# Stick-breaking attention in a two-layer transformer: VectorE and the DMA queue keep the program's order, filler steps are spread over the last units, and one more key tile is loaded before the next stage

## The chip, the core and the metric

The kernel runs on one core of a Trainium2 chip. The metric is device microseconds of one execution. A core has five engines with an instruction queue each: TensorE (PE in the profile; PEld is its weight load), VectorE (DVE), ScalarE (ACT), GpSimd (POOL) and SyncE (SP), which here issues nearly all transfers. Each engine takes its instructions in the order in which they stand in its queue; an instruction that must wait holds up those behind it on the same engine.

## What is computed

Two transformer layers on 2048 tokens of width 1024, float32. The first layer mixes three kinds of heads: six of stick-breaking attention, six of differential attention, four that attend to a memory of 256 rows. The second has sliding-window attention and memory attention. Each layer ends with a gated output projection and a layer norm. The part at issue is stick-breaking attention, here in the reference's words:

```python
def one_block(bi):
    qi = lax.dynamic_slice_in_dim(q, bi * BLOCK, BLOCK, axis=1)
    z = jnp.einsum('bqhd,bkhd->bhqk', qi, k, preferred_element_type=jnp.float32) * scale
    q_idx = bi * BLOCK + jnp.arange(BLOCK, dtype=jnp.int32)
    strict = key_idx[None, :] < q_idx[:, None]
    log_1mb = jnp.where(strict, jax.nn.log_sigmoid(-z), 0.0)
    rc = jnp.flip(jnp.cumsum(jnp.flip(log_1mb, axis=-1), axis=-1), axis=-1)
    after = rc - log_1mb
    w = jnp.where(strict, jnp.exp(jax.nn.log_sigmoid(z) + after), 0.0)
    return jnp.einsum('bhqk,bkhd->bqhd', w.astype(v.dtype), v)
```

A key's weight is its own sigmoid times the product of (1 - sigmoid) over all keys between it and the query. The kernel computes that product as a running product from the last key to the first.

## The kernel before, in words

The stages follow each other: projections of layer 1 (`layer1_proj`), stick-breaking, differential attention (`differential`), the output projection, layer 2.

**Units.** Stick-breaking works on three pairs of heads (p), for each on four chunks of 512 queries (t = 3, 2, 1, 0), and in a chunk on blocks of 128 queries against up to 512 keys. One block against one stretch of keys, for both heads of the pair, is a unit; there are 120. `begin` runs at a chunk's first unit: it loads the chunk's gate (`sl`), the next chunk's queries (`qs`) and, once per pair, the next pair's keys and values (`kv`, three tiles per pair).

**One unit.** `scores`: TensorE multiplies queries and keys into PSUM (`psz`). `weights`: ScalarE takes the two sigmoids (tiles `s` and `wb`), VectorE runs the product scan for each head (`row`), GpSimd multiplies `wb` by it. `turn`: TensorE transposes `wb` into PSUM (`pstp`, two buffers), and the result is copied to `wT`, in turn two copies by ScalarE and one by VectorE. `values`: TensorE multiplies `wT` with the values (`pspv`). The main loop for unit k writes: scores of unit k+3, turn of unit k, weights of unit k+3, and, every second k, the values of two units that were turned before. At a chunk's end VectorE multiplies with `sl` and a store writes `m1` (short: m).

**The filler.** The six stick-breaking heads' and memory heads' share of the output projection is spread over the differential stage as filler. Its first list of steps makes ready: load(0) (mp tile of m1), five loads of w_out parts (`rx`, three buffers), five `wsplit` (ScalarE casts rx into `wo`, GpSimd subtracts for the low part), split(0) and load(1). Thirteen steps in all. `begin` runs them when p = 2 and t = 1 (`FT`), fifteen units before the stage's end, and then loads the differential stage's first queries (`qa`) and keys (`kc`, tile number c for keys 512c on).

**What sets the order.** A scheduler reorders the instructions of each engine by its own model of time, except those that a `PinnedCore` marks to keep the program's order. In stick-breaking TensorE and ScalarE are so marked; VectorE, GpSimd and SP are not. While the filler's first steps are recorded, `self.nc = nc` takes the mark off for all engines. The differential stage marks TensorE and ScalarE.

**Memory.** A tile tag has a fixed number of buffers in a pool; a new tile waits until the oldest one's last user is done. Pools that are opened after others were closed lie where those lay.

Of the kernel before, what the change touches and what calls it, by code (L numbers as in the profile page):

```python
# [15 lines left out]
S = 2048  # L16
D = 1024
# [49 lines left out]
class Net:  # L67
# [152 lines left out]
    def load_x(self, between):  # L220

        nc = self.nc
        self.xs = []
        for t in range(NT):
            row = []
            for h in range(2):
                tag = "kv" if 2 * t + h < 3 else "qs" if t < 2 else "big"
                hi, lo = (self.t(tag, F32R, [P, 2048]) for _ in range(2))
                n = 1024 if t or h else 512
                for c in range(0, 2048, n):  # L230
                    raw = self.t("w")[:, :n]
                    self.dma(raw, self.i["xT"][t, h, :, c:c + n])
                    nc.scalar.copy(hi[:, c:c + n], raw)
                    nc.vector.tensor_sub(lo[:, c:c + n], raw, hi[:, c:c + n].bitcast(F32))
                    for f in between.get((t, h, c), ()):
                        f()
                row.append((hi, lo))
            self.xs.append(row)
# [290 lines left out]

    def load_sb(self, p):  # L530

        ks = [self.t("kv", F32R) for _ in range(2)]
        n = S if p else TC
        for lo in range(S - n, -1, -n):
            for hh in range(2):
                for part in range(2):
                    self.dma(ks[hh][64 * part:64 * part + 64, lo:lo + n], self.sbk[p][part, 64 * hh:64 * hh + 64, lo:lo + n])
        vp = self.t("kv", F32, [P, NB, P])
        self.dma(vp, self.v1[:, :, p * P:(p + 1) * P].rearrange("b k f -> k b f"))
        return ks, vp  # L540

    def stick_breaking(self):
# [1 line left out]


        nc = self.nc
        self.nc = pinned = PinnedCore(nc, self.tc, ("tensor", "scalar"))
        chunks = [(p, t) for p in range(3) for t in range(NT - 1, -1, -1)]
        units = [(p, t, qi, c) for p, t in chunks for qi in range(3, -1, -1) for c in range(t, -1, -1)]
        kv, qs, sls, prs, zs, ws, wTs, pvs = {0: self.sb_first[:2]}, {(0, NT - 1): self.sb_first[2]}, {}, {}, {}, {}, {}, {}  # L550
# [1 line left out]
        def begin(p, t):  # L552
            sls[p, t] = self.load_silu(self.silu[p], t)
            k = chunks.index((p, t)) + 1
            if k < len(chunks):
                qs[chunks[k]] = self.load_qstack(self.sbq[chunks[k][0]], chunks[k][1])
            if t == NT - 2 and p < 2:
                kv[p + 1] = self.load_sb(p + 1)
            if p == 2 and t == FT:
                self.fill = self.filler()  # L560
                self.nc = nc
                for f in next(self.fill):
                    f()
                self.nc = pinned
                self.dk, self.dq = {}, {}
                self.load_dq(0, 0, 0)
                for c in range(NT - 1):
                    self.load_dk(0, c)

        def bounds(u):  # L570
# [23 lines left out]
        def weights(u):  # L594
# [6 lines left out]
            self.nc.scalar.activation(w[:, :, :m], z[:, :, :m], AF.Sigmoid, scale=0.125)  # L601
            for hh in range(2):
                prr = prs[p, t, qi][hh]
                nc.vector.tensor_tensor_scan(  # L604
                    prr[:, lo + s0 - 1:hi - 1][:, ::-1], rest[:, hh, s0:m][:, ::-1], zero.to_broadcast([P, m - s0]),
                    prr[:, hi - 1:hi], ALU.mult, ALU.add)
                nc.gpsimd.tensor_mul(w[:, hh, :m], w[:, hh, :m], prr[:, lo:hi])  # L607
# [6 lines left out]
        def values(u):  # L614
# [8 lines left out]
                                          wT[hh][:, j * P:(j + 1) * P], start=(hi == n and j == 0), stop=(c == 0 and j == nj - 1))  # L623
            if qi == 0 and c == 0:
                mt = self.t("c2")
                nc.vector.tensor_mul(mt, pvs.pop((p, t)), sls.pop((p, t)))
                self.dma(self.m1[p, :, t * TC:(t + 1) * TC], mt, nc.scalar if p == 2 and t == 0 else None)

        done = 0
        zero = self.psum("zero")[:, :1]  # L630
        nc.vector.memset(zero, 0.0)
        for u in units[:SB_AHEAD]:
# [2 lines left out]
        for k, u in enumerate(units):  # L635
# [2 lines left out]
            turn(u)  # L638
            if k + SB_AHEAD < len(units):
                weights(units[k + SB_AHEAD])  # L640
            while k - done >= SB_GROUP or k == len(units) - 1 and done <= k:
                for v in units[done:done + SB_GROUP]:
                    values(v)
# [3 lines left out]
    def differential(self):  # L647
# [21 lines left out]
                f()  # L669
            del steps[:k]  # L670

        self.load_dk(0, NT - 1)
        for c in range(NT):
            self.load_dv(0, c)
        for s in range(-2, len(units)):
# [735 lines left out]

    def run(self):
        nc, dr, i = self.nc, self.dr, self.i
        with self.phase({"kv": 6, "qs": 2}, {}):
            with self.phase({"big": 8, "w": 13, "c2": 9, "mv": 2}, {"mm": 3, "z": 2, "tp": 2, "pv": 1}):
                self.layer1_proj()
            right = ExitStack()
            right.enter_context(self.phase({"rx": 3, "mp": 5, "wo": 5, "kc": 3, "qa": 2}, {}, "right"))
            with self.phase({"row": 4, "wb": 4, "s": 3, "wT": 7, "c2": 2, "sl": 2}, {"z": 2, "tp": 2, "pv": 1, "zero": 1}, "right"):
                self.stick_breaking()  # L1420
        self.rp = dr.tile([NB, P, D], F32, name="rp")
        self.silu2 = [dr.tile([P, S], F32, name=f"silu2_{f}") for f in range(8)]
        self.m2 = dr.tile([8, P, S], F32, name="m2")
        with self.phase({"c2": 3, "sl": 2}, {}):
            with self.phase({"qd": 2, "wT": 7, "vc": 4, "row": 9, "kd": 3},
                            {"mm": 1, "z": 3, "tp": 2, "pv": 2}):
                tail = self.differential()
            right.close()
            with self.phase({"big": 16}, {}):
                with self.phase({"w": 4, "raw": 1}, {"mm": 5, "tp": 3}):  # L1430
# [85 lines left out]
```

## Time and profile before

| | |
|---|---|
| Median of 3 runs | 2563.76 us (2556.67 to 2565.95) |
| Profiled execution, its own time | 2562.38 us |
| Its span, first to last instruction | 2560.5 us |
| TensorE busy | 2394.9 us, 94% |
| VectorE busy | 1572.5 us, 61% |
| ScalarE busy | 1253.9 us, 49% |
| GpSimd busy | 942.9 us, 37% |
| Mean transfer rate | 122 GB/s |

Stick-breaking takes 720 to 1082 us of the span, differential attention about 1082 to 1640. A timeline row reads: start, duration (us), engine, source line, operation, tile written <- tiles read, shape, how many; in brackets the idle time before it and what ended it. A row of stretches gives, for each engine, the busy microseconds and in parentheses the number of instructions, then the granted TensorE clock, the share of time that the DMA engines are busy, and GB/s. A row of waits names engine and tile that waited, what it waited for, then microseconds in total, times, longest. L57 is the line of the helper that marks an instruction; such instructions are told apart by their tiles.

### The profile page before, as it was taken

What the parts mean: (1) busy time and instruction counts of PE and PEld (TensorE: products, weight loads), DVE (VectorE), ACT (ScalarE), POOL (GpSimd) and SP (SyncE); (2) the same over time, 40 slices, a digit from 0 to 9 for tenths busy, and PEclk for the clock granted to TensorE, in tenths of its full rate; (3) what the DMA queues carried; (4) which work ended last, traced back from release to release, by engine and by line L of the source; (5) the groups of instructions that cost most, each with busy time, mean ns of one, the idle gap of its engine ahead of it and who ended that gap; (6) DMA issues with size and microseconds to landing.
All of it is one profiled execution on the core that took longest, in us unless ns stands there. A gap on an engine that the chain in (4) does not pass through costs nothing. (4 is left out here: it accounts for less than half of the span.)

```text
span 2560.5 us, 42280 instructions
## 1 busy us (share of the span) xinstructions
PE 2394.9 (94%) x15564; PEld 1942.7 (76%) x15564; DVE 1572.5 (61%) x3657; ACT 1253.9 (49%) x2453; POOL 942.9 (37%) x800
## 2 busy tenths in 40 slices
PE   8999999999969999879888888999999999999998
PEld 7778998888848777657666666778788777777887
DVE  4833222431149888789898999685312776677455
ACT  4442222221138788657687677543212777776100
POOL 0401003750038778610121122374621655534333
PEclk9999999999989999989899999999999999999999
DMA  8643222331481422263534341563323555533541
GB/s 291 205 159 128 81 85 85 126 132 47 122 205 43 108 67 54 64 171 97 129 99 112 94 104 54 173 212 110 87 91 114 154 161 154 145 98 103 197 143 64
DMA packets 199247, 311.60 MB, mean 122 GB/s; under 512 B 17920, under 2 KB 97280, under 8 KB 198528
## 3 DMA queue, kind: packets, MB, share of 16 engines
q1 hardware_dynamic: 198464, 307.83, 40.7%
q8 instruction: 124, 2.03, 0.3%
q10 hardware_dynamic: 576, 1.05, 0.1%
q14 instruction: 83, 0.68, 0.1%
HBM read 204.74 MB, written 104.07 MB: 121 GB/s over the span
## 5 line engine op out<-in xcount | busy, mean ns | idle before, releaser
L57 PE MATMUL psmm<-big,w 128*128 128x512 f32 x1680 | 414.5, 394 | 0.0
L57 PEld LDWEIGHTS psmm<-big,w 128*128 128x128 f32 x1680 | 306.1, 189 | 57.8
L57 ACT COPY wT<-pstp 128x512 f32<-128x512 f32 (+3 forms) x400 | 203.2, 525 | 190.9 <-PE pstp L57 186.6
L607 POOL TENSOR_TENSOR wb<-wb,row 128x512 f32<-128x512 f32 (+3 forms) x240 | 262.5, 1119 | 69.0 <-DVE row L604 49.1
L604 DVE TENSOR_TENSOR_SCAN row<-s,row,pszero 128x512 f32<-128x512 f32 (+5 forms) x240 | 252.2, 1102 | 38.8 <-ACT s L57 37.2
L254 PE MATMUL psmm<-big,w 128*128 128x512 f32 x1200 | 275.2, 389 | 0.0
L254 PEld LDWEIGHTS psmm<-big,w 128*128 128x128 f32 x1200 | 225.0, 188 | 47.0 <-issue 0.2
L57 PE MATMUL psmm<-big,mp 128*128 128x512 f32 x1056 | 244.9, 392 | 1.4 <-POOL big L1011 1.4
L57 ACT ACTIVATE row<-row,mn 128x2048 f32<-128x2048 f32 (+7 forms) x192 | 229.7, 1201 | 12.0 <-DVE mn L777 8.4
L57 PEld LDWEIGHTS psmm<-big,mp 128*128 128x128 f32 x1056 | 198.4, 189 | 42.9 <-POOL big L1011 1.8
L771 DVE TENSOR_SCALAR_CACHE_REDUCE row<-psz 128x512 f32<-128x512 f32 (+1 forms) x324 | 200.5, 639 | 30.6 <-PE psz L57 29.8
L1230 DVE TENSOR_TENSOR c<-psmm,c 128x512 f32<-128x512 f32 x62 | 42.7, 691 | 238.6 <-ACT c L1229 238.5
L941 POOL TENSOR_TENSOR mp<-mp,mp 128x640 fp32r<-128x640 f32 x32 | 53.3, 1667 | 357.4 <-ACT mp L57 268.9
L57 PE MATMUL psz<-kv,qs 128*128 128x512 f32 (+3 forms) x480 | 134.9, 399 | 17.7 <-ACT wb L57 17.4
L57 PE MATMUL psmm<-wo,mp 128*128 128x512 f32 x480 | 148.1, 421 | 3.5 <-ACT mp L57 2.8
L813 DVE SCALAR_TENSOR_TENSOR row<-row,tiny,row 128x128 f32<-128x128 f32 (+7 forms) x144 | 149.8, 1089 | 0.4
L209 POOL TENSOR_TENSOR w<-w,w 128x1024 fp32r<-128x1024 f32 x20 | 48.7, 2437 | 257.1 <-ACT w L208 156.4
L1229 ACT ACTIVATE c<-psmm 128x512 f32<-128x512 f32 x62 | 36.8, 596 | 212.5 <-PE psmm L254 204.2
L57 PE MATMUL pstp<-ident,wb 128*128 128x128 f32 x816 | 117.3, 278 | 24.9 <-DVE wT L125 13.8
L57 PE MATMUL pstp<-ident,row 128*128 128x128 f32 x816 | 131.0, 282 | 7.0 <-ACT wT L57 6.2
L57 PEld LDWEIGHTS pstp<-ident,wb 128*128 128x128 f32 x816 | 92.9, 142 | 45.1 <-POOL wb L607 25.1
L1187 ACT ACTIVATE e<-e,tiny 128x256 f32<-128x256 f32 (+1 forms) x192 | 94.6, 494 | 60.4 <-DVE e L1185 59.8
(220 smaller groups left out, 4923.0 us busy)
## 6 DMA issues: line engine op xcount, KB each, us to landing
silu<-c SPq DMA_DIRECT2D x54, 256.0 KB, 2.3
sl<-silu SPq DMA_DIRECT2D x54, 256.0 KB, 3.2
qs<-sbq SPq DMA_DIRECT2D x48, 256.0 KB, 5.3
cs<-rope SPq DMA_DIRECT2D x24, 512.0 KB, 4.3
kc<-k SPq DMA_DIRECT2D x36, 320.0 KB, 5.0
w<-in_we_dram SPq DMA_DIRECT2D x20, 512.0 KB, 3.7
raw<-in_wo_dram SPq DMA_DIRECT2D x20, 512.0 KB, 4.0
rx<-in_x_dram SPq DMA_DIRECT2D x32, 256.0 KB, 2.8
```

The lines of the kernel that those rows point to most:

```text
L57: return self.tc.keep_in_program_order(f(*a, **k))
L209: eng.tensor_sub(lo[:, sl], raw[:, sl], hi[:, sl].bitcast(F32))
L254: self.nc.tensor.matmul(ps, w[a][:, c, :], self.xpart(t, c, b), start=(c == k == 0), stop=(c == 7 and k == 2))
L604: nc.vector.tensor_tensor_scan(prr[:, lo + s0 - 1:hi - 1][:, ::-1], rest[:, hh, s0:m][:, ::-1], zero.to_broadcast([P, m - s0]), prr[:, hi ...
L607: nc.gpsimd.tensor_mul(w[:, hh, :m], w[:, hh, :m], prr[:, lo:hi])
L771: nc.vector.tensor_scalar(e[:, col + lo:col + lo + n0], z[:, :n0], -scale, before, ALU.mult, ALU.min, accum_out=acc)
L813: self.nc.vector.scalar_tensor_tensor(x[:, lo:hi], y[:, lo:hi], cf[hh][:, w:w + 1], x[:, lo:hi], ALU.mult, ALU.add)
L941: self.nc.gpsimd.tensor_sub(ml, m, mh.bitcast(F32))
L1187: nc.scalar.activation(e[:, hh, ns:], e[:, hh, ns:], AF.Exp, bias=nmx[:, hh:hh + 1], scale=-1.0, accum_out=s[:, hh:hh + 1])
L1229: nc.scalar.activation(sg, ps, AF.Sigmoid)
L1230: nc.vector.tensor_mul(sg, ps, sg)
```

## The change

It has four parts. (1) In stick-breaking SP and VectorE keep the program's order too; the scans, the last product and the copies go through `self.nc`. (2) The filler's first steps are recorded under that mark: four (load(0) and three rx loads) at `begin`, the other nine one by one after units 110 to 118. (3) The differential stage's fourth key tile is loaded by `begin` with the other three; for that its tag `kd` gets its pool before the first stage, and pair 1 of stick-breaking keeps its keys and values in it, so `kv` has three buffers in place of six. (4) `c2` and `sl` are opened once around both stages in place of one pair of pools in each.

```diff
@@ load_x
-                tag = "kv" if 2 * t + h < 3 else "qs" if t < 2 else "big"
-                hi, lo = (self.t(tag, F32R, [P, 2048]) for _ in range(2))
+                tags = {0: ("kv", "kv"), 1: ("kv", "kd"), 2: ("kd", "kd"), 3: ("qs", "qs")}.get(2 * t + h, ("big", "big"))
+                hi, lo = (self.t(tag, F32R, [P, 2048]) for tag in tags)
@@ load_sb
-        ks = [self.t("kv", F32R) for _ in range(2)]
+        tag = "kd" if p == 1 else "kv"
+        ks = [self.t(tag, F32R, [P, S]) for _ in range(2)]
...
-        vp = self.t("kv", F32, [P, NB, P])
+        vp = self.t(tag, F32, [P, NB, P])
@@ stick_breaking
-        self.nc = pinned = PinnedCore(nc, self.tc, ("tensor", "scalar"))
+        self.nc = PinnedCore(nc, self.tc, ("sync", "tensor", "vector", "scalar"))
...
                 self.fill = self.filler()
-                self.nc = nc
-                for f in next(self.fill):
+                steps.extend(next(self.fill))
+                for f in steps[:4]:
                     f()
-                self.nc = pinned
+                del steps[:4]
                 self.dk, self.dq = {}, {}
                 self.load_dq(0, 0, 0)
-                for c in range(NT - 1):
+                for c in range(NT):
                     self.load_dk(0, c)
...
-                nc.vector.tensor_tensor_scan(
+                self.nc.vector.tensor_tensor_scan(
...
-                nc.vector.tensor_mul(mt, pvs.pop((p, t)), sls.pop((p, t)))
+                self.nc.vector.tensor_mul(mt, pvs.pop((p, t)), sls.pop((p, t)))
...
+            if u[0] == 2 and k > len(units) - 11:
+                for f in steps[:1]:
+                    f()
+                del steps[:1]
@@ differential
-        self.load_dk(0, NT - 1)
@@ run
-        with self.phase({"kv": 6, "qs": 2}, {}):
...
-            with self.phase({"row": 4, "wb": 4, "s": 3, "wT": 7, "c2": 2, "sl": 2}, {"z": 2, "tp": 2, "pv": 1, "zero": 1}, "right"):
...
         with self.phase({"c2": 3, "sl": 2}, {}):
-            with self.phase({"qd": 2, "wT": 7, "vc": 4, "row": 9, "kd": 3},
+            keys = ExitStack()
+            keys.enter_context(self.phase({"kd": 3}, {}))
+            with self.phase({"kv": 3, "qs": 2}, {}):
...
+                with self.phase({"row": 4, "wb": 4, "s": 3, "wT": 7}, {"z": 2, "tp": 2, "pv": 1, "zero": 1}, "right"):
+                    self.stick_breaking()
...
+            with self.phase({"qd": 2, "wT": 7, "vc": 4, "row": 9},
```

How instructions move, at three places. First ScalarE at the start of stick-breaking (`s` and `wb` are the sigmoids, `wo` the filler's casts). Before:

```order
L57 ACTIVATE s_5942<-psz_5937 128x1024
L57 ACTIVATE wb_5944<-psz_5937 128x1024
L920 CAST wo_9768<-rx_9762 128x512
L920 CAST wo_9773<-rx_9764 128x512
L920 CAST wo_9778<-rx_9766 128x512
L57 ACTIVATE s_5955<-psz_5950 128x1024
L57 ACTIVATE wb_5957<-psz_5950 128x1024
L57 COPY wT_5973<-pstp_5968 128x512
```

Now, of the same units:

```order
L57 ACTIVATE s_5945<-psz_5940 128x1024
L57 ACTIVATE wb_5947<-psz_5940 128x1024
L57 ACTIVATE s_5958<-psz_5953 128x1024
L57 ACTIVATE wb_5960<-psz_5953 128x1024
L57 COPY wT_5976<-pstp_5971 128x512
```

The three casts (two more stood some rows on) are gone from here. They now stand at the end of the stage, the fourth and fifth like this, each behind the sigmoids of one of the last two units:

```order
L57 ACTIVATE s_10201<-psz_10180 128x2x256
L57 ACTIVATE wb_10203<-psz_10180 128x2x256
L57 CAST wo_10209<-rx_10055 128x512
L57 COPY wT_10228<-pstp_10223 128x512
L57 ACTIVATE s_10237<-psz_10216 128x2x128
L57 ACTIVATE wb_10239<-psz_10216 128x2x128
L57 CAST wo_10245<-rx_10132 128x512
```

Second SP's queue at the end of the stage, from the last load of queries (`qs`) on. Before:

```order
L113 DMA qs_9754<-sbq_228 64x2x512 x4
L113 DMA m_246<-c_1769_9959 128x512
L113 DMA sl_10107<-silu_242 128x512
L113 DMA m_246<-c_1840_10257 128x512
L113 DMA kd_10357<-dfk_235 32x4x512 x4
L113 DMA vc_10362<-v_239 128x4x128
```

Now, from the same load on (two rows of mp and two more of rx stand between the first and the second, and one more qa and two more kc are left out):

```order
L57 DMA qs_9757<-sbq_237 64x2x512 x4
L57 DMA rx_9769<-in_woute_dram 128x512
L57 DMA qa_9776<-dfq_241 32x4x256 x4
L57 DMA kc_9791<-dfk_244 32x4x512 x4
L57 DMA kd_9796<-dfk_244 32x4x512 x4
L57 DMA m_255<-c_1761_9941 128x512
L113 DMA kd_11131<-dfk_245 32x4x512 x4
L113 DMA kd_11136<-dfk_245 32x4x512 x4
L57 DMA rx_10055<-in_woute_dram 128x512
L57 DMA sl_10097<-silu_251 128x512
L57 DMA rx_10132<-in_woute_dram 128x512
```

The filler's and the differential stage's first loads now stand here; before they stood at the start of stick-breaking, and three of the rx at the very head of the program's queue. The two groups of kd from dfk_245 are keys of the differential stage's second pair, which the scheduler moves this far up because `kd` now has free buffers. Behind the second rx come three loads of x, a store of m, mp, sl, the four vc, eight qd and the next mp.

Third VectorE, for units near the start (a scan reads `s`, a copy writes `wT`). Before:

```order
L604 SCALAR_TENSOR_TENSOR row_5918<-s_5955,row_5918,pszero_5909 128x512
L604 SCALAR_TENSOR_TENSOR row_5919<-s_5955,row_5919,pszero_5909 128x512
L125 COPY wT_6006<-pstp_6001 128x512
L604 SCALAR_TENSOR_TENSOR row_5918<-s_5982,row_5918,pszero_5909 128x511
L604 SCALAR_TENSOR_TENSOR row_5919<-s_5982,row_5919,pszero_5909 128x511
```

Now:

```order
L57 SCALAR_TENSOR_TENSOR row_5921<-s_5958,row_5921,pszero_5912 128x512
L57 SCALAR_TENSOR_TENSOR row_5922<-s_5958,row_5922,pszero_5912 128x512
L57 SCALAR_TENSOR_TENSOR row_5921<-s_5985,row_5921,pszero_5912 128x511
L57 SCALAR_TENSOR_TENSOR row_5922<-s_5985,row_5922,pszero_5912 128x511
L57 COPY wT_6009<-pstp_6004 128x512
```

The copy has moved behind the next unit's two scans. So it is for 21 of the stage's 80 copies on VectorE; the others keep their place. TensorE's order is the same throughout.

More of the change, by code (lines that the diff above doesn't have):

```diff
@@ L625, in values @@
                 mt = self.t("c2")
-                nc.vector.tensor_mul(mt, pvs.pop((p, t)), sls.pop((p, t)))
+                self.nc.vector.tensor_mul(mt, pvs.pop((p, t)), sls.pop((p, t)))
                 self.dma(self.m1[p, :, t * TC:(t + 1) * TC], mt, nc.scalar if p == 2 and t == 0 else None)
-        done = 0
+        done, steps = 0, []
         zero = self.psum("zero")[:, :1]
@@ L1413, in run @@
         nc, dr, i = self.nc, self.dr, self.i
-        with self.phase({"kv": 6, "qs": 2}, {}):
[L1415 to L1418, printed above, removed]
-            with self.phase({"row": 4, "wb": 4, "s": 3, "wT": 7, "c2": 2, "sl": 2}, {"z": 2, "tp": 2, "pv": 1, "zero": 1}, "right"):
[L1420 to L1423, printed above, removed]
-        with self.phase({"c2": 3, "sl": 2}, {}):
-            with self.phase({"qd": 2, "wT": 7, "vc": 4, "row": 9, "kd": 3},
+        with self.phase({"c2": 3, "sl": 2}, {}):
+            keys = ExitStack()
+            keys.enter_context(self.phase({"kd": 3}, {}))
+            with self.phase({"kv": 3, "qs": 2}, {}):
+                with self.phase({"big": 8, "w": 13, "c2": 9, "mv": 2}, {"mm": 3, "z": 2, "tp": 2, "pv": 1}):
+                    self.layer1_proj()
+                right = ExitStack()
+                right.enter_context(self.phase({"rx": 3, "mp": 5, "wo": 5, "kc": 3, "qa": 2}, {}, "right"))
+                with self.phase({"row": 4, "wb": 4, "s": 3, "wT": 7}, {"z": 2, "tp": 2, "pv": 1, "zero": 1}, "right"):
+                    self.stick_breaking()
+            self.rp = dr.tile([NB, P, D], F32, name="rp")
+            self.silu2 = [dr.tile([P, S], F32, name=f"silu2_{f}") for f in range(8)]
+            self.m2 = dr.tile([8, P, S], F32, name="m2")
+            with self.phase({"qd": 2, "wT": 7, "vc": 4, "row": 9},
                             {"mm": 1, "z": 3, "tp": 2, "pv": 2}):
                 tail = self.differential()
+            keys.close()
             right.close()
```

## The prediction

> **What bounds the kernel now.** I read the stretches first, cut where the program changes stage, to see where TensorE is not full.
>
> ```profile
> core 0: us, PE busy (x) PEld busy (x) DVE busy (x) ACT busy (x) POOL busy (x), PEclk, DMA share, GB/s
> 360.00:720.00 360.00, 360.00 (x1824) 304.66 (x1823) 101.31 (x171) 70.88 (x129) 104.79 (x62) 1.00 0.34 109
> 720.00:760.00 40.00, 17.87 (x102) 13.22 (x100) 16.58 (x17) 15.61 (x21) 18.41 (x20) 0.71 0.99 233
> 880.00:920.00 40.00, 38.22 (x374) 31.52 (x375) 37.38 (x41) 33.04 (x48) 33.54 (x39) 1.00 0.17 41
> 1085.00:1120.00 35.00, 24.00 (x79) 17.02 (x80) 20.42 (x74) 11.91 (x20) 4.07 (x3) 0.80 0.95 218
> ```
>
> Stick-breaking runs from 720 to 1082 us. Well inside it TensorE is busy 38.2 of 40 us, so TensorE bounds it, with VectorE close behind at 37.4. There are two holes: its first 40 us (17.9 busy) and the 35 us behind its end (24.0 busy). Both have the transfers full (0.99 and 0.95). I then read each hole in order of time, with what each instruction had waited for in brackets. The first:
>
> ```profile
> 726.38 1.04 PE L57 MATMUL pstp<-ident,wb 128*128 128x128 f32 x8
> 739.54 1.66 ACT L920 CAST wo<-rx 128x512 fp32r<-128x512 f32 x3 [14.23 <-DMA m<-c]
> 743.08 1.01 PE L57 MATMUL psz<-kv,qs 128*128 128x384 f32 x2 [15.66 <-ACT wb L57]
> 755.16 0.62 ACT L920 CAST wo<-rx 128x512 fp32r<-128x512 f32 x1 [6.32 <-DMA rx<-in_woute_dram]
> 760.10 0.62 ACT L920 CAST wo<-rx 128x512 fp32r<-128x512 f32 x1 [2.00 <-DMA rx<-in_woute_dram]
> ```
>
> These are the filler's five weight casts, not stick-breaking's own work. ScalarE runs its instructions in order, so for 14.23 + 6.32 + 2.00 = 22.6 us it stood before them, and the sigmoids and copies that TensorE needs stood behind them. The transfers they waited for were late in a queue that also carried the next stage's keys and queries. The second hole:
>
> ```profile
> 1041.73 3.31 SPq L113 DMA_DIRECT2D qs<-sbq  x4
> 1074.48 0.60 ACT L57 ACTIVATE wb<-psz 128x512 f32<-128x512 f32 x1
> 1081.50 0.88 PE L57 MATMUL pspv<-wT,kv 128*64 128x128 f32 x12
> 1089.65 0.77 PE L57 MATMUL psz<-kd,qa 128*128 128x512 f32 x1 [5.68 <-DMA kd<-dfk]
> 1114.08 0.72 ACT L57 CAST mp<-mp 128x640 fp32r<-128x640 f32 x1 [8.12 <-DMA mp<-m]
> 1117.60 0.17 DVE L802 RECIPROCAL tiny<-tiny 128x2 f32<-128x2 f32 x1 [5.09 <-ACT row L57]
> ```
>
> The fourth key tile costs TensorE 5.68 us. A filler load that came late (8.12 us for ScalarE) costs VectorE 5.09 us soon after.
>
> **The change, part by part.** Sums are made against the profiled execution, 2562.4 us (span 2560.5, so 1.9 lie around it); the median shown, 2563.8, is 1.4 above it.
>
> *Kernel start.* Three loads of woute leave the head of the queue.
>
> ```profile
> 1.16 1.37 SPq L113 DMA_DIRECT2D rx<-in_woute_dram  x3
> 2.00:4.00 2.00, 0.00 (x0) 0.00 (x0) 0.02 (x1) 0.62 (x2) 0.00 (x0) 1.00 0.87 281
> 8.94 15.83 PE L57 MATMUL psmm<-kv,w 128*128 128x512 f32 x60 [8.94 <-ACT kv L233]
> rx<-in_woute_dram SPq DMA_DIRECT2D x3, 256.0 KB, 4.7
> ```
>
> They are 0.79 MB ahead of the first x tile, and 0.79 / 281 GB/s is **2.8 us**. TensorE is full behind them until 720, so the gain carries. Bounds: 0, if the later x tiles set the pace anyway, and 4.2 (the 1.37 of issue added).
>
> *First hole.* The casts go to the stage's end, the keys and queries with them. The 17.87 us of TensorE work take 18.7 at the pace of 38.22 in 40; I add 2.8 us for filling the pipeline, in which VectorE's scans pace the first units, and get 21.5 in place of 40: **18.5 us** gained. Bounds: 21.3 (no fill), and 14.9 (the fill costs all of the 6.4 us up to the first transposes, at 726.4).
>
> *The middle.* VectorE's transpose copies now stand where they are written. 21 of the 80 lose a place ahead of two scans; the other 59 stand as they are.
>
> ```profile
> DVE wT L125 <- PE pstp L57: 15.6, 17, 1.7
> PE pstp L57 <- DVE wT L125: 13.0, 24, 1.5
> PEld pstp L57 <- POOL wb L607: 22.1, 27, 2.1
> ```
>
> These are the waits from 770 to 1070. Set against the order, 15 of the 17 VectorE waits, and nearly all of the 15.6 us, stand before the early copies; no wait of TensorE stands behind one. TensorE's 13.0 us all stand behind the 54 later copies of this stretch, 0.24 us each. So the 21 moved ones would cost TensorE 21 x 0.24 = 5 us. Against that, VectorE gets back up to 15.6 us, and TensorE's waits for GpSimd's products, which follow the scans, are 22.1. Bounds: 5 lost, and 13 gained, if every wait of TensorE for a copy went. Between them I take **2 us** gained, near zero because TensorE is already 95% busy.
>
> *The end.* This is where I forecast a loss. From the last query load on, SP now issues in a row: four qs, mp, three rx, eight qa, twelve kc, four kd, a store, eight more kd, and only then the rx of the fourth weight cast.
>
> ```profile
> qs<-sbq SPq DMA_DIRECT2D x8, 256.0 KB, 9.6
> qa<-dfq SPq DMA_DIRECT2D x8, 128.0 KB, 5.5
> kc<-dfk SPq DMA_DIRECT2D x12, 256.0 KB, 8.3
> 10.00:15.00 5.00, 5.00 (x17) 3.98 (x17) 3.65 (x6) 3.73 (x6) 0.00 (x0) 1.00 1.04 413
> 1079.14 1.82 SPq L113 DMA_DIRECT2D kd<-dfk  x4
> 1086.40 8.90 SPq L113 DMA_DIRECT2D qd<-dfq  x8
> ```
>
> With kd as large as kc and mp at 320 KB by its shape, that is 1024 + 320 + 768 + 1024 + 3072 + 1024 + 256 + 2048 + 256 = 9792 KB, 10.0 MB. The first hole moved the same mixture at 233 GB/s, so it takes 43 us from 1041.7 and lands at 1085. The cast is queued right behind the sigmoid that ended at 1075.1. ScalarE therefore waits 10 us, with the last units' copies and sigmoids behind it. Bounds on the rate: 413 GB/s (the x tiles) lands it at 1066, no wait; kd, vc and qd, 3.1 MB issued from 1079.1 to 1095.3, make 194, and a wait of 18.
>
> ```profile
> L920 ACT CAST wo<-rx x5: 613/617/617, 739.5 to 760.1; 128x512 fp32r<-128x512 f32 x5
> L921 POOL TENSOR_TENSOR wo<-rx,wo x5: 1267/1272/1284, 740.2 to 760.8; 128x512 fp32r<-128x512 f32 x5
> 1079.14 0.46 POOL L607 TENSOR_TENSOR wb<-wb,row 128x128 f32<-128x128 f32 x1 [0.19 <-DVE row L604]
> L941 POOL TENSOR_TENSOR mp<-mp,mp 128x640 fp32r<-128x640 f32 x32 | 53.3, 1667 | 357.4 <-ACT mp L57 268.9
> ```
>
> After that the chain goes over GpSimd: the fifth rx (0.5 MB behind, 2.3 us), its cast 0.6 and subtraction 1.3 to 1089.1, then in GpSimd's order products of about 0.7 and 0.46, the mp subtraction 1.67 and a last product 0.46, to 1092.4; transposes, a copy and the last values (0.44 + 0.29 + 0.88) end at 1094.0. Before, they ended at 1082.4: **11.6 us** lost. The fourth key tile is then there: **5.7** gained. The eight kd out of the way should take off half of VectorE's 5.09, but the new mp loads stand behind vc and qd: **2.5** gained (bounds 0 and 5.1). The end nets a loss of 3.4.
>
> The Trainium skill, "DMA: Bandwidth & Descriptors", section Specifications, puts what a core draws from HBM at about 358 GB/s. By it the 10.0 MB would land at 1070, ahead of the cast, and the time would be that of the first rival below. The trace does not hold to it either way: 233 in this mixture, 413 for the x tiles.
>
> Sum: -2.8 - 18.5 - 2 + 3.4 = -19.9; 2562.4 becomes 2542.5, and on the scale of the median 2563.8 becomes **2544**.
>
> **Rivals.**
>
> 1. *The queue drains in time.* For it: 413 GB/s above. Against it: 233 in just this mixture. Only the filler's added GpSimd work remains (5 x 1.27 + 1.67, of which I count 3 us): -2.8 - 18.5 - 2 + 3 - 5.7 - 5.1 = -31.1, **2533**.
> 2. *The moved copies cost without a return.* +5 in the middle in place of -2: -12.9, **2551**. For it: TensorE waits only behind late copies. Against it: VectorE's 15.6 us.
> 3. *The first hole stays.* Another wait takes the casts' place, for example stick-breaking's own row or weight tiles on buffers that the first stage still stores from. Then 18.5 falls away: -1.4, **2562**, no change. Against it: nothing but the casts waited for a transfer there.
> 4. *Slower: VectorE's program order itself.* Each moved copy lets TensorE stand for 1.5 us, the longest single wait behind a late copy, in place of 0.24: 21 x 1.5 = 31.5. Sum -2.8 - 18.5 + 31.5 + 3.4 = +13.6, **2577**. It decides from 0.85 us a copy on; the mean against it is 0.24.
>
> **How the numbers follow.** Forecast 0.53 (its own range, from the rates and the middle, 2536 to 2554); rival 1 0.18; rival 2 0.12; rival 3 0.11; rival 4 0.06. The range that should hold 8 in 10 reaches from below rival 1 to past rival 2, **2530 to 2557**. A difference of 0.5%, 13 us, is about what a measurement of this kernel tells from none: faster by more, below 2551, is 0.49 of the forecast's chance, all of rival 1 and half of rival 2: 0.73. Slower is rival 4 and a sliver of rival 3: 0.07. Between lie 0.20.
>
> **What would show it.** First matmul near 6 us, not 8.94. From 717 to 757, TensorE busy over 33 of 40 us, and no ScalarE cast of wo there. At the end, a cast of wo on ScalarE that waited some 10 us for rx, close before the last values; no wait of TensorE for kd. In the middle, fewer waits of VectorE for transposes and more of TensorE for VectorE's copies. The forecast is wrong if the first 40 us still stand at half, if no late cast waits (rival 1), or if TensorE's waits for copies pass 20 us (rivals 2 and 4).

## The result, and the profile after

The changed kernel takes 2545.55 us (median of 5 runs, 2543.03 to 2546.44); the kernel before, in the runs beside it, 2557.58. The ratio is 0.9936, with a 95% interval from 0.9919 to 0.9952: 0.64% faster. It is not the quotient of the two medians, which is 0.9953, 12 us; the five runs of the kernel before lie 9.5 us apart. The forecast was 2544, 0.9923 of the time before. The profiled execution of the changed kernel took 2546.16 us with a span of 2544.4, so 16.1 us of span were won against the profile before, where the sum had 19.9.

The same stretches as before, of the changed kernel, cut where its stages now change (columns as before):

```profile
core 0: us, PE busy (x) PEld busy (x) DVE busy (x) ACT busy (x) POOL busy (x), PEclk, DMA share, GB/s
720.00:757.00 37.00, 32.36 (x292) 25.95 (x292) 32.88 (x36) 30.16 (x43) 28.51 (x30) 1.00 0.17 45
1040.00:1080.00 40.00, 23.71 (x203) 18.97 (x202) 17.27 (x34) 17.10 (x32) 21.41 (x29) 0.79 0.93 218
1080.00:1120.00 40.00, 31.75 (x110) 21.67 (x109) 36.33 (x110) 21.40 (x35) 6.25 (x4) 0.90 0.53 151
```

The first hole is gone: TensorE is busy 32.4 of 37 us where it had 17.9 of 40. There is a new hole at the stage's end, 23.7 of 40, in a queue that is full (0.93). The places in it, from the changed kernel's timeline in order of time:

```profile
5.54 8.13 PE L57 MATMUL psmm<-kv,w 128*128 128x512 f32 x25 [5.54 <-ACT kv L233]
101.01 11.22 PE L57 MATMUL psmm<-big,w 128*128 128x512 f32 x48 [1.31 <-ACT c L325]
...
1018.34 3.59 SPq L57 DMA_DIRECT2D qs<-sbq  x4
1048.27 8.82 SPq L113 DMA_DIRECT2D kd<-dfk  x8
1051.08 0.60 ACT L57 ACTIVATE wb<-psz 128x512 f32<-128x512 f32 x1
1057.96 0.35 SPq L57 DMA_DIRECT2D rx<-in_woute_dram  x1
1067.02 0.62 ACT L57 CAST wo<-rx 128x512 fp32r<-128x512 f32 x1 [15.34 <-DMA rx<-in_woute_dram]
1068.27 0.87 PE L57 MATMUL pstp<-ident,wb 128*128 128x128 f32 x3 [14.08 <-ACT wT L57]
1075.23 0.89 PE L57 MATMUL pspv<-wT,kv 128*64 128x128 f32 x12
1077.54 0.49 PE L57 MATMUL psz<-kd,qa 128*128 128x512 f32 x1
```

The fourth weight cast stood 15.34 us in ScalarE's order, right behind the sigmoid at 1051, for the rx load that SP issued behind the eight kd loads. TensorE stood 14.08 us behind the copy that came after that cast. The fourth key tile (1077.54) waits for nothing any more; it had cost 5.68.

Where the 16.1 us came from is read by laying the traces side by side, the same instruction in each. Six marks serve here and below: the first transpose of stick-breaking; its 69th value matmul (behind the first hole); its 1565th (ahead of the end); its last of 1632; the first transpose of the differential stage; that stage's last value matmul. In microseconds against the kernel before:

| | first transpose | behind first hole | ahead of the end | last values | differential, first transpose | its last values | whole span |
|---|---|---|---|---|---|---|---|
| before, at | 726.4 | 769.0 | 1071.1 | 1082.1 | 1132.1 | 1635.7 | 2560.5 |
| changed | -0.5 | -23.7 | -23.4 | -6.3 | -14.9 | -19.5 | -16.1 |

So the first hole gave 23.2, the middle nothing (0.3 lost), the end took 17.1 back, the opening of the differential stage gave 8.6, the rest of that stage 4.6, and 3.4 were lost behind it.

### The profile page after: what moved, and what is told of

The parts are those of the page before. It is cut to its first block, busy times and chain, and to the rows that moved or that the text cites. A ratio compares the mean times of both kernels' runs of the same rounds, so it can differ in the third digit from the quotient of the medians.

```text
span 2544.4 us, 42300 instructions
## 1 busy us (share of the span) xinstructions
PE 2392.6 (94%) x15564; PEld 1939.8 (76%) x15564; DVE 1573.6 (62%) x3657; ACT 1254.2 (49%) x2453; POOL 939.3 (37%) x800
## 5 line engine op out<-in xcount | busy, mean ns | idle before, releaser
L57 PEld LDWEIGHTS pstp<-ident,row 128*128 128x128 f32 x816 | 99.6, 143 | 30.8 <-ACT wT L57 13.4
```

The lines of the kernel that those rows point to most:

```text
L57: return self.tc.keep_in_program_order(f(*a, **k))
```

## The experiments

Twelve kernels were run, each beside the kernel before on the same chip. The marks of each profiled execution:

| | ratio, 95% interval | first transpose | behind first hole | ahead of the end | last values | differential, first transpose | its last values | span |
|---|---|---|---|---|---|---|---|---|
| changed kernel | 0.9936 [0.9919, 0.9952] | -0.5 | -23.7 | -23.4 | -6.3 | -14.9 | -19.5 | -16.1 |
| spread only | 0.9918 [0.9904, 0.9933] | 1.6 | -23.1 | -24.9 | -22.4 | -22.3 | -25.6 | -25.2 |
| no spread | 0.9931 [0.9916, 0.9946] | 0.6 | -20.0 | -18.4 | -18.4 | -26.9 | -26.0 | -22.3 |
| fourth key late | 0.9898 [0.9882, 0.9915] | -0.3 | -23.5 | -23.1 | -19.2 | -28.5 | -32.8 | -29.8 |
| weights early | 0.9917 [0.9898, 0.9935] | -1.0 | -24.1 | -22.4 | -22.5 | -24.1 | -24.0 | -20.3 |
| VectorE free | 0.9943 [0.9928, 0.9958] | 0.4 | -24.3 | -26.2 | -9.9 | -20.0 | -22.4 | -18.7 |
| SP free | 0.9910 [0.9892, 0.9927] | 2.9 | -20.2 | -19.9 | -16.1 | -25.5 | -22.9 | -19.3 |
| both | 0.9894 [0.9876, 0.9911] | -0.8 | -23.9 | -22.2 | -22.2 | -28.6 | -30.7 | -27.7 |
| both, VectorE free | 0.9894 [0.9878, 0.9909] | -1.6 | -26.3 | -26.7 | -26.7 | -32.8 | -31.7 | -28.0 |
| late key, pools' order | 0.9886 [0.9864, 0.9908] | -0.5 | -23.7 | -23.3 | -18.4 | -27.5 | -30.3 | -27.3 |
| all | 0.9896 [0.9871, 0.9921] | -2.0 | -26.7 | -27.2 | -27.2 | -34.7 | -38.8 | -35.1 |
| late key, large buffers moved | 0.9967 [0.9956, 0.9979] | -1.6 | -24.7 | -24.4 | -20.4 | -28.4 | -34.3 | -14.6 |
| the same, VectorE free | 0.9950 [0.9935, 0.9964] | -0.7 | -25.3 | -27.2 | -24.7 | -32.6 | -37.6 | -14.5 |

The marks are one execution each. Executions of one kernel differ by up to 10 us (those of "late key, large buffers moved" took 2547.7 to 2557.8), those of the kernel before by up to 12. "All" and "late key, large buffers moved" were profiled in their fastest execution, "weights early" and "SP free" in their slowest (2541.98 and 2543.02, with medians of 2539.04 and 2537.06). The profile before, 2562.38, is slower than the medians that the ratios stand beside, 2557.58 to 2561.60. So a mark tells where time goes, and the ratio how much.

### What removes the first hole

**Spread alone.** The kernel before, with the filler's first steps spread; SP, VectorE, pools and the fourth key as they were:

```diff
             if p == 2 and t == FT:
                 self.fill = self.filler()
-                self.nc = nc
-                for f in next(self.fill):
-                    f()
-                self.nc = pinned
+                steps.extend(next(self.fill))
+                for f in steps[:4]:
+                    f()
+                del steps[:4]
...
+            if u[0] == 2 and k > len(units) - 11:
+                for f in steps[:1]:
+                    f()
+                del steps[:1]
```

> The kernel before with one part of the change: the filler's first steps are spread over the last units (four at the second-last chunk, one at each unit from the 111th on); SP and VectorE stay free, pools and the fourth key tile as before. Theory (the first hole is the five weight casts standing in ScalarE's order, and moving them is enough): the hole of 23 us goes, TensorE is busy over 30 of the 37 us from 720; SP, being free, still issues three rx loads at the kernel's start and the keys early, so no cast waits over 2 us at the end; about 2 us are lost to the casts and subtractions there. 2557 - 23 + 2 = 2536, ratio 0.992. Rival (the queue itself, full of the next stage's keys and queries, makes the hole, and SP's program order is what cured it): stick-breaking's own loads wait in the casts' place, the hole stays above 12 us, 2545 to 2557, ratio over 0.995.

2538.08 us, ratio 0.9918: as the theory had it. Its stretch, and the last three weight casts of its timeline:

```profile
720.00:757.00 37.00, 33.87 (x289) 27.02 (x289) 32.22 (x36) 29.62 (x42) 27.66 (x31) 1.00 1.02 232
...
1047.76 0.67 ACT L57 CAST wo<-rx 128x512 fp32r<-128x512 f32 x1
1050.03 0.63 ACT L57 CAST wo<-rx 128x512 fp32r<-128x512 f32 x1
1052.04 0.63 ACT L57 CAST wo<-rx 128x512 fp32r<-128x512 f32 x1
```

The queue is as full as it was (1.02 of the time, 232 GB/s), and TensorE works through it, since nothing of stick-breaking stands behind a late transfer. At the end no cast waits.

**No spread.** The changed kernel, with the filler's steps free at one place as before:

```diff
-                steps.extend(next(self.fill))
-                for f in steps[:4]:
-                    f()
-                del steps[:4]
+                pinned, self.nc = self.nc, nc
+                for f in next(self.fill):
+                    f()
+                self.nc = pinned
```

> The changed kernel with the filler's thirteen first steps recorded at one place and free, as before; SP and VectorE in program order, early keys. The casts then stand at stick-breaking's start on ScalarE again, but the keys and queries of the next stage do not stand in the queue there. Theory (the place of the casts makes the hole): the three first casts still wait for the stores of the stage before, whose buffers they take, and the last two for their loads; the hole is back with 10 to 23 us; at the end no late cast, 15 us gained back. Sum with the changed kernel 2545 + 17 - 15 = 2547, ratio 0.992 to 0.998. Rival (the full queue makes the hole): under 5 us of hole, 2530, ratio 0.990 or less.

2540.77 us, ratio 0.9931. Here the theory fell and the rival was right on the hole; the time lies between the two, and that the ratio falls into the theory's bounds is chance. The same stretch, and the five casts:

```profile
720.00:757.00 37.00, 30.23 (x257) 23.32 (x256) 29.80 (x32) 30.23 (x42) 31.04 (x31) 1.00 0.32 86
...
725.72 1.68 ACT L924 CAST wo<-rx 128x512 fp32r<-128x512 f32 x3
732.34 0.62 ACT L924 CAST wo<-rx 128x512 fp32r<-128x512 f32 x1 [0.30 <-POOL wo L925]
734.73 0.63 ACT L924 CAST wo<-rx 128x512 fp32r<-128x512 f32 x1
```

The casts stand at the stage's start, as they did before, and wait 0.30 us in place of 22.6. With SP in the program's order the next stage's keys and queries do not stand in the queue there (0.32 of the time). The largest of the old waits, 14.23 us, was for a store (m<-c), not for a load. The last store of the stage before, in the kernel before and in this one:

```profile
733.97 0.34 SPq L113 DMA_DIRECT2D m<-c  x1
723.04 0.33 SPq L113 DMA_DIRECT2D m<-c  x1
```

The casts of the kernel before start at 739.5, those of this one at 725.7, each behind that store. In the kernel before eight loads of qs and five of kv, stick-breaking's own later ones, and three of qa are issued ahead of it from 698 us on; here five of qs. So the hole needed both, the casts early on ScalarE and a full queue ahead of the transfers they wait for; taking away either was enough. One rival is left: this run has the new pools too, by which other tiles lie under the casts' buffers. SP's order alone, on the kernel before, was not run. Against the spread, casts there cost some 3 us behind the first hole and 5 ahead of the end; the spread pays 4 of these back in the last units.

### What makes the new hole

**Fourth key late.** The load of the key tile goes back to where it was written before:

```diff
-                for c in range(NT):
+                for c in range(NT - 1):
                     self.load_dk(0, c)
...
+        self.load_dk(0, NT - 1)
         for c in range(NT):
             self.load_dv(0, c)
```

> The changed kernel with the load of the fourth key tile written in the next stage again. The scheduler then puts the three loads of that tile and of the next pair's first two keys (12 transfers, 3.1 MB) ahead, behind the 100th unit, so that they no longer stand between the keys and the fourth weight load. Theory (that load is late because of the bytes queued ahead of it): 10.0 MB become 6.6 MB, at the 10 MB in 25 us that the changed kernel's trace showed some 9 us earlier, and at the prediction's 233 GB/s 14 us; the cast's wait of 15.3 falls to 1 to 6 us, no key waits, and the time falls by 9 to 14 us to 2532 to 2537, ratio 0.990 to 0.992. Rival (the weight load waits for its buffer or for its place in SP's order, whatever is ahead): the wait stays above 10 us and the time within 4 us of the changed kernel, 0.9936.

2532.28 us, ratio 0.9898: the theory, from the bytes, at the lower edge of its times, though no cast waits, where it had 1 to 6 us left. (Its first rate, 10 MB in 25 us, was misread: the changed kernel's trace has 10.7 MB in the 48.7 us from the first query load to the landing.) From its timeline:

```profile
939.30 5.31 SPq L113 DMA_DIRECT2D kd<-dfk  x8
952.65 3.84 SPq L113 DMA_DIRECT2D kd<-dfk  x4
...
1043.14 0.35 SPq L57 DMA_DIRECT2D rx<-in_woute_dram  x1
1049.59 0.68 ACT L57 CAST wo<-rx 128x512 fp32r<-128x512 f32 x1
1051.86 0.63 ACT L57 CAST wo<-rx 128x512 fp32r<-128x512 f32 x1
1053.87 0.63 ACT L57 CAST wo<-rx 128x512 fp32r<-128x512 f32 x1
```

The rx load is issued at 1043.1 in place of 1058.0, no cast waits, the last values come 12.9 us earlier. The key tile is not late either: it lies in the `kd` pool now, which pair 1 leaves empty, and the scheduler, free to move that load, issues it from 939 us on by itself, with the next pair's first two tiles (the twelve kd rows). It was the mark on SP that held it behind the kc loads, and the eight further kd loads behind it.

**Weights early.** The three first weight loads a chunk earlier, casts and the other two loads at units 96 to 102, the first mp load ahead of the queries and keys; the key loads stay:

```diff
+            if p == 2 and t == NT - 2:
+                self.fill = self.filler()
+                steps.extend(next(self.fill))
+                first.append(steps.pop(0))
+                for f in steps[:3]:
+                    f()
+                del steps[:3]
             if p == 2 and t == FT:
-                self.fill = self.filler()
-                ...
+                first.pop()()
...
-            if u[0] == 2 and k > len(units) - 11:
+            if k in (95, 96, 97, 98, 99, 100, 101, 117, 118):
```

> The changed kernel with the filler's weights one chunk earlier: the three first loads at the start of the third-last chunk, casts and the last two loads at units 96 to 102, the first mp load ahead of the next stage's queries and keys; the last two steps stay at units 118 and 119. All 12 key transfers with the fourth key tile stay behind. Theory (the stage's end was lost to one cast behind the keys' bytes): no cast waits over 2 us, the last values come 20 to 22 us before those of the kernel before, the next stage opens as in the changed kernel: 2545 - 14 = 2531, ratio 0.989 to 0.991. Rival (the jam moves on: the keys, the second mp load or the x tiles land late, and the next stage's scores or ScalarE's next cast wait in its place): 2538 or more, ratio over 0.992.

2539.04 us, ratio 0.9917. Both were half right: the last values come 16.2 us earlier than in the changed kernel, and then 7.0 of it are gone at the differential stage's first transpose, where the jam has moved on to the filler's mp tile (4.7 more go within that stage, which is another matter, see below):

```profile
1049.45 6.79 SPq L113 DMA_DIRECT2D kd<-dfk  x7
1057.19 0.34 SPq L57 DMA_DIRECT2D m<-c  x1
1059.70 1.39 SPq L57 DMA_DIRECT2D mp<-m  x2
1068.33 0.72 ACT L57 CAST mp<-mp 128x640 fp32r<-128x640 f32 x1 [8.96 <-DMA m<-c]
```

The kd loads now delay the store of m, the mp load behind it, and with that ScalarE by 8.96 us at the opening of the next stage. The cause of the end's loss is the bytes in SP's queue; the weight cast is only the first to stand behind them.

**SP free.** The changed kernel with SP unmarked:

```diff
-        self.nc = PinnedCore(nc, self.tc, ("sync", "tensor", "vector", "scalar"))
+        self.nc = PinnedCore(nc, self.tc, ("tensor", "vector", "scalar"))
```

> The changed kernel with SP taken out of the program order in stick-breaking; spread filler, VectorE's order and the new pools stay. Theory, as the first four runs left it (either the spread or SP's order is enough against the first hole; SP's order together with the spread makes the late weight cast): first hole as small as in the changed kernel, no cast that waits over 3 us at the end, first matmul back at 9 to 10 us, VectorE's order costs its 2.8 us, the stage's last values at 20 to 22 us before those of the kernel before in place of 6.3, and the next stage opens without the wait for its fourth key: 2530 to 2535, ratio 0.989 to 0.991. Rival (the pools and the early key tile are what jams the end): as the changed kernel, 2544, 0.9936.

2537.06 us, ratio 0.9910: 2 us above the times expected, and the last values come 16.1 us before those of the kernel before, not 20 to 22; 2.9 of that is a later start. No cast waits at the end, the next stage gains 9.4 at its opening, and the three rx loads are back at the kernel's head, as the first matmul shows:

```profile
9.59 2.80 PE L57 MATMUL psmm<-kv,w 128*128 128x512 f32 x5 [9.59 <-ACT kv L233]
```

What they cost at stick-breaking's start is of the size in which the kernels differ there anyway: those with that head reach the first transpose at 0 (the kernel before), 0.6, 1.6 and 2.9, those without at -2.0 to 0.4.

### VectorE's order

**VectorE free.** The changed kernel with VectorE unmarked:

```diff
-        self.nc = PinnedCore(nc, self.tc, ("sync", "tensor", "vector", "scalar"))
+        self.nc = PinnedCore(nc, self.tc, ("sync", "tensor", "scalar"))
```

> The changed kernel with VectorE taken out of the program order again (21 copies of stick-breaking may go ahead of the scans once more). Theory (the moved copies cost and gain nothing that lasts, since the middle ran within 0.3 us of the kernel before): within 3 us of the changed kernel, ratio to the kernel before 0.993 to 0.995; the end's wait of 15 us stays. Rival 1 (the program order of VectorE costs 5 us that something else hid): 2540, ratio 0.9915. Rival 2 (it is what keeps the middle at pace): 2555 or more, ratio over 0.998.

2543.78 us, ratio 0.9943: not to be told from the changed kernel. The marks show more than the time. Without the order the middle keeps the pace of the kernel before; behind the first hole it is 0.6 us ahead of the changed kernel, ahead of the end 2.8. The waits of the same stretch of the middle, of the kernel before, of the changed kernel and of this one (what waited, for what, total us, times, longest):

```profile
PE pstp L57 <- DVE wT L125: 10.9, 20, 1.5
DVE wT L125 <- PE pstp L57: 13.3, 15, 1.7
DVE row L604 <- ACT s L57: 12.3, 20, 1.7
```

```profile
PE pstp L57 <- DVE wT L57: 11.1, 20, 1.5
DVE row L57 <- ACT s L57: 27.6, 30, 2.2
DVE wT L57 <- PE pstp L57: 0.5, 1, 0.5
```

```profile
DVE wT L125 <- PE pstp L57: 13.2, 15, 1.7
DVE row L605 <- ACT s L57: 12.3, 20, 1.7
```

VectorE's waits for transposes went, 13.3 to 0.5, and came back as waits of its scans for ScalarE's sigmoids, 12.3 to 27.6. TensorE waits for VectorE's copies as long as before, 11.1 us after 10.9.

**Both, with VectorE in order and free.** The two edits against the jam together (the diffs of "fourth key late" and "weights early"), and then the mark on VectorE taken off as above:

> The weights one chunk earlier, and the load of the fourth key tile written in the next stage, so that the scheduler puts it ahead of the jam. Theory (both lift the same wait): hardly better than either alone, 2528 to 2532, ratio 0.988 to 0.990. Rival (each lifts a loss of its own): 2520 or less, ratio under 0.986.

> The same, with VectorE out of the program order. Theory (VectorE's order costs about 2.8 us in the middle, as the run without it showed unit by unit): 2.8 us less than the kernel with both, ratio lower by 0.001. Rival (what is gained in the middle is waited for at the stage's end): the same time as with both.

2533.21 and 2533.32 us, 0.9894 each. Both edits lift one loss, as the theory had it: the differential stage's first transposes come at -28.6, as with the late key alone (-28.5). VectorE's freedom gains 4.5 us ahead of the end and is 1.0 ahead at the differential stage's last values; nothing is left in the time, as the rival had it.

### The 3 us behind the differential stage

Every kernel with the new pools and the large buffers where they were loses 3.0 to 3.7 us between the differential stage's last values and the end of the span; spread alone, with the pools of before, loses 0.4. In the kernel before, VectorE's weight casts for the next projection waited only for their loads; in the changed kernel the second waits 12 us for the stage's last transposes, and TensorE then waits for GpSimd's half of the weights. The rows of the kernel before, and of the changed one:

```profile
1626.49 0.69 DVE L1009 CAST big<-rx 128x1024 fp32r<-128x1024 f32 x1 [4.52 <-DMA rx<-in_woute_dram]
1638.28 11.86 PE L57 MATMUL psmm<-big,mp 128*128 128x512 f32 x51 [1.38 <-POOL big L1011]
```

```profile
1613.21 1.29 DVE L1013 CAST big<-rx 128x1024 fp32r<-128x1024 f32 x2 [11.98 <-PE pstp L57]
1620.78 13.36 PE L57 MATMUL psmm<-big,mp 128*128 128x512 f32 x51 [3.37 <-POOL big L1015]
```

In the built program, that second cast's buffer lies over the differential stage's kd tiles before, and over one of its last row tiles now. Two layouts were tried on the kernel with the late key; two further runs join them with VectorE free, the first of these, "all", with the weights early as well.

```diff
-            with self.phase({"qd": 2, "wT": 7, "vc": 4, "row": 9},
+            with self.phase({"wT": 7, "vc": 4, "row": 9, "qd": 2},
```

> The kernel with the fourth key tile's load written late, and the pools of the differential stage opened in another order (the query tiles last), so that the second weight cast of the stage behind it takes a buffer whose last reader is a score matmul well ahead of the stage's end, in place of the last transposes. Theory (3.0 to 3.7 us are lost between the differential stage's last values and the end in every kernel with the new pools, 0.4 in the one with the old ones, since that cast waits for the transposes): the cast waits under 1 us for TensorE, the tail is 3 us shorter, 2529, ratio 0.988 to 0.989. Rival (the next cast or a load takes over the wait): as with the late key alone, 2532, 0.990.

> The weights one chunk earlier, the fourth key tile's load written late, VectorE out of the program order, and that order of the pools. Theory (the gains of layout and place add, the one of VectorE's freedom is lost again in the next stage, where VectorE is the bound): 2530, ratio 0.988 to 0.989, no better than the late key with the pools' order. Rival (they all add up): 2525 or less, ratio 0.987 or less.

2531.90 (0.9886) and 2534.08 (0.9896). The edit did not do what it was for:

```profile
1602.44 1.29 DVE L1014 CAST big<-rx 128x1024 fp32r<-128x1024 f32 x2 [11.98 <-PE pstp L57]
```

The cast waits the same 11.98 us. The buffer still reached over the same row tile, which had moved with it, as the built program's addresses told afterwards. So this run says nothing of the cause, and the two kernels stand with those they were made from.

```diff
-            with self.phase({"big": 16}, {}):
+            with self.phase({"big": 16}, {}, "right"):
```

> The kernel with the fourth key tile's load written late, and the 16 large buffers of the last stages laid on the other side of the memory. In the built program the second weight cast's buffer then lies over mp and rx buffers of the filler in place of the last row tile (the pools' order tried before had left it over that row tile). Theory (in the kernels with the new pools that cast waits 12 us for the last transposes, and 3.0 to 3.7 us are lost between the differential stage's last values and the end): no weight cast on VectorE waits over 5 us, TensorE's wait for GpSimd's big tile falls from 3.4 to 1.8 us or less, the loss behind the last values falls to 0 to 1 us; against the late key alone 3 us less, 2529, ratio 0.988 to 0.989. Rival (another tile or load of the new layout is late in its place): 2532 or more, loss behind the last values still 3 us.

> The same, with VectorE out of the program order. Theory (its order costs 2.8 us in the middle, and in the two pairs of runs so far nothing of it was left in the time): within 2 us of the kernel with the large buffers on the other side, last values of stick-breaking 3 us earlier. Rival (with the tail mended it is left over): 3 us less, 2526, ratio 0.987.

2551.63 (0.9967) and 2548.90 (0.9950), 0.7 and 0.5% of the time more than the late key alone. VectorE's freedom, 2.8 us ahead of the end, shows in the time by 0.17%, with intervals that overlap: between theory and rival, and not settled. For the large buffers the rival held:

```profile
1604.37 1.11 DVE L1014 CAST big<-rx 128x1024 fp32r<-128x1024 f32 x1 [18.57 <-DMA rx<-in_woute_dram]
```

No cast waits for transposes now, but the first one waits 18.57 us for its load, and TensorE 3.9 for that cast. From the last values of the differential stage to 1655 us this kernel loses 5 us on the one with the late key; the greater loss lies further back, and is told of in the last section. That the row tile under the cast's buffer costs the 3 us is thus read from the traces and not shown by an experiment.

## Why the prediction was right

The time came to 2545.55 for a forecast of 2544, by the forecast's own case: a first hole that goes, and a late weight cast at the end that takes some of it back. Its terms, against the traces:

- **Kernel start, -2.8: measured -0.5** at the stage's start. The first matmul came at 5.54 where the text said near 6, 3.4 earlier than before; 2.5 of it held until 98 us. There TensorE waited 1.31 for ScalarE's `c` tile (the row at 101.01), whose chain had gained only half a microsecond. The step that failed is "TensorE is full behind them until 720": the row for it began at 360. The lower bound, 0, was the better choice.
- **First hole, -18.5: measured -23.2,** above the upper bound of 21.3. The mechanism held, and no cast is there. Two sizes were off. The stretch was closed at 760, with the last cast; the 35th transpose, at which the two kernels are compared here, came 1.4 us later. And the 17.87 us of TensorE work had been read at a granted clock of 0.71. From the stage's first matmul to that transpose, in the kernel before and in the changed one:

```profile
720.21:761.60 41.39, 18.14 (x104) 13.33 (x102) 16.58 (x17) 17.11 (x25) 19.21 (x21) 0.71 0.96 225
719.66:737.80 18.14, 14.65 (x103) 10.84 (x102) 16.27 (x17) 14.64 (x20) 13.82 (x14) 1.00 0.36 94
```

  At the full clock the same matmuls are busy 14.65 us. At the pace of 38.22 in 40 that is 15.3, where the sum had 18.7; the 2.8 put down for filling the pipeline is just what is left of the 18.1.
- **The middle, -2: measured +0.3.** The step that failed is "VectorE gets back up to 15.6 us": it did, and stood for the sigmoids instead. Unit by unit VectorE's order cost 2.2 us up to 1019, as it does against the run without it: on the losing side, where the value taken was a gain, and half the bound of 5. A jump of -1.9 at 1029, in all kernels with the spread over the last units, hides it: there the kernel before had the filler's first mp cast, which had waited 1.92 us for its load.
- **The end, +3.4: measured +8.5** (17.1 for 11.6 on the last values, 8.6 for 8.2 at the opening of the next stage). Right in mechanism, place and nearly in rate, as the two stretches between the first query load and the landing show:

```profile
1018.00:1041.00 23.00, 21.18 (x206) 17.08 (x205) 20.81 (x22) 19.10 (x29) 17.86 (x22) 1.00 0.95 209
1041.00:1067.00 26.00, 11.92 (x128) 9.70 (x126) 11.12 (x14) 9.63 (x18) 13.22 (x20) 0.82 1.06 230
```

  At 209 and 230 GB/s that is 10.7 MB in 48.7 us, where the sum had 10.0 MB at 233 in 43. The five to six us more are the 15.34 us of wait in place of 10, and the 17.1 in place of 11.6.
- **Not in the sum:** 4.6 gained within the differential stage and 3.4 lost behind it. The first goes with the granted clock. The stretch between that stage's two marks, in the kernel before and in the changed one:

```profile
1132.00:1636.00 504.00, 443.94 (x3378) 343.26 (x3376) 448.82 (x1364) 362.81 (x661) 75.88 (x49) 0.96 0.39 105
1117.00:1616.00 499.00, 438.81 (x3373) 339.27 (x3372) 447.40 (x1364) 362.57 (x660) 75.11 (x47) 0.97 0.39 106
```

  As many matmuls keep TensorE busy 5.1 us less. Over the other kernels the term lies between 5.9 gained and 2.6 lost: the stretch takes 499 us at 0.97 with the late key, 505 at 0.95 without the spread, 506 at 0.96 with SP free. Spread alone, 500 at 0.96, shows that the clock is not all of it, and what lowers the clock in one execution and not in another is not shown. So these 4.6 us cannot be put down to the change.

The nearness is luck, twice. The misses nearly cancel: 4.7 too little at the first hole, 2.3 too much each at the start and in the middle, 5.1 too little lost at the end, 1.2 for the rest. And the kernel before had a median of 2557.58 beside the changed one, where the forecast counted from 2563.8: the same 19.9 taken off 2557.58 would have been 2537.7. The time was better than its terms.

**The rivals.** Rival 1 (the queue drains in time) was not the case. Its 2533 is near the 2532.3 that the kernel took with the late load out of the jam, by the same mis-sized terms for the start and the first hole. Rival 2 (moved copies cost without a return) had the middle right, at half its size. Rival 3 fell with the first stretch. Rival 4 needed 0.85 us for each moved copy; TensorE's waits for copies came to 11.1 us where they had been 10.9. The page of the Trainium skill that was weighed, "DMA: Bandwidth & Descriptors", section Specifications, with its 358 GB/s would, by an estimate from that figure, have had the load land ahead of the cast. The rows above say 209 to 230 for this mixture.

**What the reasoning lacked** is what the first two runs told: the hole had two conditions, and the change removed both. I gave all of it to the moved casts. Seen as two, the spread gains little beside SP's order as far as stick-breaking goes: against "no spread", the kernel with the late key is 0.8 us ahead at the last values and 1.6 at the differential stage's first transpose. Their times lie 8.5 us apart (2540.77 and 2532.28), with intervals that do not touch, but 5.2 of that arise within the differential stage, at 0.95 and 0.97 of the clock in the two profiles, and the two differ in the key load besides; what the spread is worth in the time is not settled. The 13 us of jam in the changed kernel are the price of the spread and of SP's order together with the marked key load. The smallest edit that lifts it keeps the spread and SP's order, and leaves the one key load unmarked: 2532.28 us, ratio 0.9898, and its interval does not touch that of the changed kernel. The next best, at 2531.90 to 2534.08, cannot be told from it.

## What to carry to other kernels

Here ScalarE stalled on late transfers where two things met: an instruction that stood early in its order, and bytes that stood ahead of its transfer in a queue. Either one removed was enough for the first hole, and the two cures together made a new one; run them apart before both are kept. Before busy time is carried over from a stretch full of waits, look at the granted clock there: at 0.71 the same matmuls were busy 18.1 us, at 1.00 14.65. When a queue is put into program order, add up the bytes ahead of the first load that an in-order engine stands behind, and divide by the rate which the trace shows for a full queue of that mixture; and of a wait that will go, ask what that engine waits for next.

## What the hardware showed that was not expected

The kernel with the moved large buffers has 15.2 us more span than the one with the late key. Apart from the 5 up to 1655 us, 7.4 are lost from 1660 to 1960 us and 5.1 from 2350 to the end, at a steady pace, with TensorE busy all the time at the full granted clock and no wait. The same stretch, first of the kernel with the late key, then with the buffers moved (the groups' columns: count, busy us and mean ns):

```profile
L254 PE MATMUL psmm<-big,w 128*128 128x512 f32 x513 | 117.0, 390 | 0.0
1770.00:1930.00 160.00, 160.00 (x719) 130.19 (x718) 36.91 (x63) 29.62 (x46) 51.95 (x34) 1.00 0.27 84
```

```profile
L254 PE MATMUL psmm<-big,w 128*128 128x512 f32 x469 | 110.1, 396 | 0.0
1770.00:1930.00 160.00, 160.00 (x703) 126.75 (x702) 38.00 (x66) 29.88 (x46) 54.36 (x36) 1.00 0.28 86
```

The same matmul takes 396 ns in place of 390, and 703 fit where 719 did. In the built programs TensorE has the same instructions, 22 of them in another place by a few; what else differs there is where tiles lie: the large ones at 98 to 229 KB of a partition in place of 15 to 146, the `w` tiles at 15 to 32 KB in place of 146 to 163. The two ran on two chips, on which the kernel before took 2559.06 and 2561.60 us, 0.1% apart; the same with VectorE free also has 396 ns, and the kernel before 390. What makes the matmul slower was not tried.
